# A two-layer hybrid decoder: first layer's split, results kept in SBUF, full-array norms, and a moved dense step

## The chip, the cores and the metric

The kernel runs on one core of a Trainium2 chip. The metric is the time of one execution in microseconds on the device, the median of several runs. The names of the engines are those of the profile: PE is TensorE's matmul, PEld its weight load, DVE is VectorE, ACT is ScalarE, POOL is GpSimd, SP is SyncE, whose queue issues most transfers.

## The reference

A trunk of two layers works on x (512 tokens of 1024 channels, float32) and a memory of 256 rows. Each layer adds two things to the running state h: a mixer of the normalised h, and a cross attention to the memory.

```python
un = rmsnorm(h, mix_norm_g[l])
z = un @ w_in[l]                     # 1024 x 10384: everything below is cut from z
y_rw  = rwkv7(token_shift(r, k, v, w_lo, a_lo), ...)   # 8 heads of 64, a state of 64 x 64 per head
y_gla = gla(q, k, v, f_lo)           # gated linear attention, 4 heads, chunks of 64, rms norm at its end
y_ret = retention(q, k, v, positions)# rotary embedding, 4 heads, layer norm at its end
y_lru = rglru(x)                     # conv of width 4 and a linear recurrence
y_n   = y_n * silu(gate_n)           # each branch has its own gate
merged = sum_n sigmoid(merge_n) * (y_n @ w_branch[l, n])
h = h + merged @ w_out[l]
h = h + cross_attention(rmsnorm(h), rmsnorm(mem))
```

In RWKV-7 the keys of each head are divided by their length, `kk / max(sqrt(sum(kk * kk)), 1e-12)`, the decay is `exp(-exp(log_w))` with `w0 + tanh(w_lo) @ w2` inside, and `a = sigmoid(a0 + a_lo @ a2)`; the codes `w_lo` and `a_lo` have 64 channels each. A last RMS norm closes the trunk.

## The kernel before

Everything is kept with channels on partitions and the 512 tokens in the free dimension, so h is eight tiles of 128 x 512 (tag `hm`). Precision is float32: each operand is split into a high part and the rest (`split`, L295, ScalarE casts and VectorE subtracts), and a product is three matmuls, high by high, high by rest and rest by high (`mm3`, L283, the matmuls of L287, L288 and L289). Weights come in pieces of 512 KB by SP's queue (`wload`, L266: tile `st`, three buffers), and are split the same way (L275 on ScalarE, L276 on VectorE). "Dense" below means these matmuls, 24 for one block of 128 output channels from 1024 (a gate or a projection), 12 from 512 (a branch's output).

The order of the instructions on every engine is made by a planner at build time: it plays the program with estimated times, takes what is ready by priority (order of the text, moved by `high_priority`), and fixes each engine's queue. `issue_after(ins)` adds an edge of order alone: what is in its block stands behind `ins` on that engine. Tiles of a tag share its buffers. PSUM has four large buffers (tag `b`, `pb`) for dense sums and four small ones (tag `s`, `pss`) for everything else.

The places that the change touches:

- Head of layer 1 (L192 to L200, L369 to L374, L349 to L359, L435 to L464). x is loaded in four pieces of 256 channels, transposed (L257), copied to `hm` (L372), squared and summed for the norm (L301 on ScalarE, L304 on POOL), multiplied by the gain (L357) and split (`gain_split`). The norm's factor r goes by a matmul with ones (L311) and a reciprocal. `proj_tok` computes values with tokens on partitions, in two halves of 264 (or 256) columns, from the split without r, and multiplies by r at the end; both halves sum in the large PSUM buffers, four token blocks each. `bcast_cols` (L335) spreads r over the partitions and `norm_split` (L338) makes the normalised split `uh`, `ul`.
- Linear attention (`gla`, L516) ends with four results, which `put_y` (L507) splits into tiles of tag `m` (eight buffers) and writes to DRAM (`y_sc`) by POOL's queue; `branch(n)` (L812) loads them back into tag `yb` (eight buffers) by the same queue. Retention and the recurrence do the same; RWKV's results are split in place.
- Retention (`ret`, L638) loads the rope tables into two tiles of tag `m` (L643, L644), projects q and k, swaps their halves by transfers within SBUF (L652, four for q, four for k), applies the rotation on VectorE (L654 to L656), and projects four gates before the keys are transposed.
- The rope tables themselves are made once (`rope_tables`, L396) in tiles of tag `yb`.
- RWKV's preparation (`rwkv_prep`, L871). The squares of the keys are summed per head by a matmul in plain float32 with a 32-column selector (L902), each of four blocks j of 128 channels into its own 32 PSUM partitions. The codes' weights and the codes are split over the two halves of the partitions; per block j two matmuls take the full 128 rows (L923), two take 64 rows for the rest (L926), and two of 32 rows (L940) spread the inverse lengths over the head's channels.
- In the same loop over j the dense work of the branches is handed out by `step(n)`: five steps ahead of the scores, one at the end (`NST = (5, 1)`). A step is a gate (24 matmuls, two gates at a branch's start) or an output (12 matmuls). The scores (L969, 32 matmuls of 64 rows) wait behind the five steps by `issue_after`; then ScalarE scales the keys' tile b2 chunk by chunk (L988, eight operations), TensorE transposes it (L257, 16 of 64 columns), ScalarE copies the result out (L996), and after that stands the one step.

```python
                for c in range(8):
                    S.mul(b2[:, c], b2[:, c], PL[:, j, c:c + 1])
                ...
                        transpose(tps[q][:, c], b2[qs, c].rearrange("p x s -> p (x s)"), ident[qs, qs])
                ...
                step(NST[1])
```

Behind it come the bonus (two matmuls, L1005) and nine transposes of the values, all into small PSUM buffers, and then the next block's codes.

## Time and profile before

| | us |
|---|---|
| median of 3 runs | 1773.82 (1769.37 to 1776.67) |
| the profiled execution | 1775.84 |
| its span, first to last instruction | 1774.1 |
| PE busy | 1735.2 |
| DVE busy | 1149.7 |
| ACT busy | 805.0 |
| POOL busy | 133.3 |

Mean granted TensorE clock 0.989 of full speed. The profile is of one execution; its span is a little shorter than the device's time for it. Matmuls overlap and their ends are modelled, so TensorE counts as busy for a little time after its last start; the distance from one start to the next tells more than one matmul's duration. The chain of work that ended last is 89% PE, 5% DVE, 3% transfers and 2% ACT.

### The profile page before, as it was taken

How to read it: one execution, taken by the hardware profiler on the slowest of the kernel's cores; microseconds unless marked ns; L12 is line 12 of the kernel's file. 1: busy time of each engine (PE TensorE's matmuls, PEld its weight loads, DVE VectorE, ACT ScalarE, POOL GpSimd, SP SyncE). 2: the span in 40 equal slices, each digit the busy share in tenths (PEclk: the TensorE clock that was granted, in tenths of full speed). 3: DMA queues.
4: the chain of work that ended last, by engine and by line, in shares of the span. 5: the costliest groups of instructions: out<-in, count | busy, mean ns of one | idle time of the engine just before them, and what ended most of it. 6: DMA issues, size and time to landing. Idle time of an engine off the chain costs nothing.

```text
span 1774.1 us, 27983 instructions
## 1 busy us (share of the span) xinstructions
PE 1735.2 (98%) x10690; PEld 1435.5 (81%) x10690; DVE 1149.7 (65%) x2376; ACT 805.0 (45%) x1507; POOL 133.3 (8%) x294
## 2 busy tenths in 40 slices
PE   6999999999999999999999999999999999999998
PEld 6987877877787788989898877787777778889898
DVE  8688576576775745756576736647766658457554
ACT  5494425444322334545447743544442224335454
POOL 2010200000002000000100101100101030000002
PEclk9999999999999999999999999999999999999999
DMA  7343735345563353424333427433537335334232
GB/s 217 108 131 96 183 100 146 95 110 158 152 160 91 99 162 98 134 88 127 112 92 89 140 64 213 125 96 99 156 97 198 102 94 171 96 96 142 72 107 84
DMA packets 333126, 217.34 MB, mean 123 GB/s; under 512 B 60512, under 2 KB 306624, under 8 KB 332992
## 3 DMA queue, kind: packets, MB, share of 16 engines
q1 hardware_dynamic: 318704, 189.72, 37.3%
q0 software_dynamic: 14288, 25.83, 5.1%
q8 instruction: 84, 1.38, 0.3%
q14 instruction: 50, 0.41, 0.1%
HBM read 180.91 MB, written 31.98 MB: 120 GB/s over the span
## 4 chain that ended last, share of the span: by engine, by line
PE 89%; DVE 5%; DMA 3%; ACT 2%; issue 1%; SPq 0%; POOL 0%; DVEq 0%; ACTq 0%; POOLq 0%
PE pb L287 26%; PE pb L288 26%; PE pb L289 25%; PE ps L257 3%; DVE wl L276 1%; DMA R<-R 1%; PE ps L287 1%; PE ps L289 1%; PE ps L1140 1%; PE ps L1122 1%; PE ps L288 1%; DMA m<-rope_sc 1%; PE ps L1128 1%; PE ps L717 0%; ACT sc L988 0%
## 5 line engine op out<-in xcount | busy, mean ns | idle before, releaser
L275 ACT CAST wh<-st 128x512 fp32r<-128x512 f32 (+1 forms) x548 | 339.7, 620 | 632.0 <-PE pb L288 493.4
L276 DVE TENSOR_TENSOR wl<-st,wh 128x512 fp32r<-128x512 f32 (+1 forms) x548 | 377.2, 690 | 342.8 <-ACT wh L275 308.1
L287 PE MATMUL pb<-uh,wh 128*128 128x512 f32 x1488 | 590.1, 397 | 0.0
L288 PE MATMUL pb<-ul,wh 128*128 128x512 f32 x1488 | 589.1, 396 | 0.0
L289 PE MATMUL pb<-uh,wl 128*128 128x512 f32 x1488 | 586.8, 394 | 0.0
L287 PEld LDWEIGHTS pb<-uh,wh 128*128 128x128 f32 x1488 | 282.1, 190 | 61.9 <-issue 3.7
L288 PEld LDWEIGHTS pb<-ul,wh 128*128 128x128 f32 x1488 | 282.0, 190 | 61.7 <-issue 3.9
L289 PEld LDWEIGHTS pb<-uh,wl 128*128 128x128 f32 x1488 | 281.7, 189 | 58.9 <-issue 1.2
L287 PE MATMUL pb<-yb,wh 128*128 128x512 f32 x256 | 102.2, 399 | 0.0
L289 PE MATMUL pb<-yb,wl 128*128 128x512 f32 x256 | 102.2, 399 | 0.0
L288 PE MATMUL pb<-yb,wh 128*128 128x512 f32 x256 | 101.4, 396 | 0.0
L288 PE MATMUL pb<-wl,R 128*128 128x264 f32 (+1 forms) x256 | 73.4, 288 | 4.3 <-DVE wl L276 4.3
L287 PE MATMUL pb<-wh,R 128*128 128x264 f32 (+1 forms) x256 | 73.1, 288 | 1.2 <-ACT wh L275 1.0
L289 PE MATMUL pb<-wh,R 128*128 128x264 f32 (+1 forms) x256 | 72.9, 290 | 1.3 <-DVE R L297 1.3
L289 PEld LDWEIGHTS pb<-yb,wl 128*128 128x128 f32 x256 | 48.3, 189 | 11.2 <-issue 0.7
L288 PEld LDWEIGHTS pb<-yb,wh 128*128 128x128 f32 x256 | 48.5, 189 | 10.1
L287 PEld LDWEIGHTS pb<-yb,wh 128*128 128x128 f32 x256 | 48.4, 189 | 10.2
L288 PEld LDWEIGHTS pb<-wl,R 128*128 128x128 f32 x256 | 49.8, 195 | 4.8 <-DVE wl L276 4.5
L287 PEld LDWEIGHTS pb<-wh,R 128*128 128x128 f32 x256 | 49.2, 193 | 2.2 <-ACT wh L275 1.3
L289 PEld LDWEIGHTS pb<-wh,R 128*128 128x128 f32 x256 | 49.2, 194 | 1.7 <-DVE R L297 1.5
L845 DVE SCALAR_TENSOR_TENSOR bt<-bt,pb 128x512 f32<-128x512 f32 x48 | 32.8, 682 | 26.3 <-PE pb L289 26.2
L257 PE MATMUL ps<-ident,R 128*128 128x128 f32 (+1 forms) x184 | 31.2, 290 | 12.0 <-DMA R<-in_x 6.8
(354 smaller groups left out, 2600.7 us busy)
## 6 DMA issues: line engine op xcount, KB each, us to landing
st<-in_w_in SPq DMA_DIRECT2D x154, 512.0 KB, 3.6
st<-in_w_branch SPq DMA_DIRECT2D x32, 512.0 KB, 3.4
st<-in_xa_wkv SPq DMA_DIRECT2D x32, 512.0 KB, 3.6
y_sc<-m POOLq DMA_DIRECT2D x48, 256.0 KB, 3.1
yb<-y_sc POOLq DMA_DIRECT2D x48, 256.0 KB, 5.5
st<-in_w_out SPq DMA_DIRECT2D x16, 512.0 KB, 3.8
st<-in_xa_wq SPq DMA_DIRECT2D x16, 512.0 KB, 4.0
st<-in_xa_wo SPq DMA_DIRECT2D x16, 512.0 KB, 4.0
```

The lines of the kernel that those rows point to most:

```text
L257: PE.transpose(o, i, idn)
L275: S.copy(hi, st[:, i * n:(i + 1) * n])
L276: V.tensor_tensor(lo, st[:, i * n:(i + 1) * n], hi.bitcast(F32), op=ALU.subtract)
L287: PE.matmul(o, ah, bh, start=first and i == 0, stop=False)
L288: PE.matmul(o, ah, bl, start=False, stop=False)
L289: last_mm[0] = PE.matmul(o, al, bh, start=False, stop=last and i == n - 1)
L845: V.scalar_tensor_tensor(th[d], th[d], 1.0, o, op0=ALU.add, op1=ALU.mult)
L1122: PE.matmul(rp[QS[q], j], LR[j][:, q, 0, cs_], SV[j // 2][:, j % 2, q, cs_], start=True, stop=True)
L1128: PE.matmul(up[QS[q], j], TT[QS[q], j, cs_], rs[QS[q], j], start=True, stop=True)
L1140: PE.matmul(sp[QS[q], j], bk[:, 2 * j + q], uv[:, q, j], start=True, stop=True)
```

## The change

- Layer 1 gets its own head, `first_rows`. x's pieces are loaded in another order, with the first two weight pieces of the first projection among them. From each transposed block in PSUM ScalarE writes gain times block as the high part, VectorE subtracts to the rest straight from PSUM and copies the block to `hm`. The transposes, the casts and VectorE's two operations are each chained in order. The norm's sum comes from 16 squares with accumulation on ScalarE, straight from x. In every layer `proj_tok` runs k by k over its four token blocks, and its second half sums in the small PSUM buffers.
- Linear attention's four results are split into `yb` tiles and stay there until branch 1 takes them. The rope tables are made in `hm` tiles instead.
- The key norms: the squares are split as other operands, and eight matmuls with the full array (`gather`) sum them into one group, high part and rest on all 128 partitions. The inverse lengths hold their high part in one half of the partitions and the rest in the other, and one full matmul per block (`spread`) spreads them. The codes' rests lie in two full tiles (of tag `uv`) with zeros in the other half, so each of four matmuls per block takes the full array.
- In the loop over j the single step is issued before the transposes of the scaled keys, which stand behind its last matmul by `issue_after`.
- The constants for these selectors change their shape, a padding tile grows, and POOL's scratch for descriptors is halved.

```diff
-    spread = p[:, None] % 32 == p[None, :] // 64
-    return np.concatenate([same, spread], 1).astype(np.float32)
+    gather = (np.arange(134)[None, :] - 6) % 64 == p[:, None] // 64
+    spread = p[:, None] % 64 == np.arange(T)[None, :] // 64
+    return np.concatenate([same, gather, spread], 1).astype(np.float32)
...
-    cp.tile([P, 64], F32, name="pad0")
+    cp.tile([P, PAD0], F32, name="pad0")
...
-        for i in range(4):
-            nc.sync.dma_start(xs[i], a["x"][:, i * 256:(i + 1) * 256].rearrange("(b p) d -> p b d", p=P))
+        load_x(0)
...
+        first_w = []
+        for q in range(2):
+            st = wp.tile([P, 4, 264], F32, tag="st", bufs=3, name=nm("st"))
+            nc.sync.dma_start(st, a["w_in"][0][q * 512:(q + 1) * 512, COL["gla_v"]:COL["gla_v"] + 264].rearrange(
+                "(k p) c -> p k c", p=P))
+            first_w.append(st)
+            for i in ((1, 2), (3,))[q]:
+                load_x(i)
...
-    heads = cp.tile([P, 2, P], F32R, name="heads")
-    G.dma_start(heads, a["heads"].rearrange("p (i c) -> p i c", i=2))
+    heads = cp.tile([P, P + 134 + T], F32R, name="heads")
+    G.dma_start(heads, a["heads"])
+    same = heads[:, 0:P]
+    def gather(j):
+        return heads[:, P + 6 - 2 * j:2 * P + 6 - 2 * j]
+    def spread(j):
+        return heads[:, (j + 1) * P + 134:(j + 2) * P + 134]
...
-    hT = [ht() for _ in range(KD)]
-    for k in range(KD):
-        tp = pss()
-        for b in range(4):
-            transpose(tp[:, b * P:(b + 1) * P], xs[k // 2][:, b, (k % 2) * P:(k % 2 + 1) * P], ident)
-        (V.tensor_copy if k % HMOD == 0 else S.copy)(hT[k], tp)
+    def first_rows(gcol):
+        hT = [ht() for _ in range(KD)]
+        gh, gl = [Rt((P, 4, T), F32R) for _ in range(2)], Rt((P, 4, T), F32R)
+        hi, lo, acts = [], [], []
+        ss = tiny(16).rearrange("p (b i) -> p b i", i=4)
+        last = {}
+        def chain(eng, f):
+            with ExitStack() as es:
+                if eng in last:
+                    es.enter_context(tc.issue_after(last[eng].ins))
+                last[eng] = f()
+            return last[eng]
+        for k in range(KD):
+            uh, ul = gh[k // 4][:, k % 4], gl[:, k] if k < 4 else yb()
+            with tc.high_priority(offset=100000):
+                tp = pss()
+                for b in range(4):
+                    chain("PE", lambda: PE.transpose(
+                        tp[:, b * P:(b + 1) * P], xs[k // 2][:, b, (k % 2) * P:(k % 2 + 1) * P], ident))
+                acts.append(chain("S", lambda: S.activation(uh, tp, AF.Copy, scale=gcol[:, k:k + 1])))
+            with tc.high_priority(offset=WPRI - 500):
+                chain("V", lambda: V.scalar_tensor_tensor(ul, tp, gcol[:, k:k + 1], uh.bitcast(F32), op0=ALU.mult,
+                                                          op1=ALU.subtract))
+                chain("V", lambda: V.tensor_copy(hT[k], tp))
+            hi.append(uh)
+            lo.append(ul)
+        for i in range(4):
+            with tc.issue_after(acts[min(2 * i + 3, KD - 1)].ins):
+                for b in range(4):
+                    jk = mt((P, 256))
+                    S.activation(jk, xs[i][:, b], AF.Square, accum_out=ss[:, b, i:i + 1])
+        r = tiny(4)
+        V.tensor_reduce(r, ss, axis=AX.X, op=ALU.add)
+        S.activation(r, r, AF.Sqrt, scale=1.0 / D, bias=epst[:, 0:1])
+        V.reciprocal(r, r)
+        return hT, hi, lo, r
...
-        pi_ = yb(I32)
+        pi_ = ht(I32)
...
-            parts = [wload(w_in[q * 512:(q + 1) * 512, col + c0:col + c0 + wd], 4, wd) for q in range(2)]
-            os_ = [pb((P, wd)) for _ in range(4)]
-            for q in range(2):
+            parts = [wload(w_in[q * 512:(q + 1) * 512, col + c0:col + c0 + wd], 4, wd, None if half else staged[q])
+                     for q in range(2)]
+            os_ = [(pss if half else pb)((P, wd)) for _ in range(4)]
+            for k in range(KD):
                 for b in range(4):
                     bs = slice(b * P, (b + 1) * P)
-                    mm3(os_[b], [(gh[k][:, bs], gl[k][:, bs], parts[q][0][k % 4], parts[q][1][k % 4])
-                                 for k in range(4 * q, 4 * q + 4)], first=q == 0, last=q == 1)
+                    mm3(os_[b], [(gh[k][:, bs], gl[k][:, bs], parts[k // 4][0][k % 4], parts[k // 4][1][k % 4])],
+                        first=k == 0, last=k == KD - 1)
...
+        kept = []
         def put_y(n, j, y):
+            if n == 1:
+                kept.append((yb(), yb()))
+                split(*kept[-1], y)
+                return
...
-                hi, lo = yb(), yb()
-                if n == 0:
+                hi, lo = kept[k] if n == 1 else (yb(), yb())
+                if n == 1:
+                    pass
+                elif n == 0:
...
-            xlo = ht(F32R)
+            xlo = [sb.tile([P, T], F32R, tag="uv", bufs=3, name=nm("uv")) for _ in range(2)]
+            for i in range(2):
+                G.memset(xlo[i].bitcast(F32)[(1 - i) * 64:(1 - i) * 64 + 64], 0.0)
             for i in range(2):
                 qs, os_ = slice(i * 64, i * 64 + 64), slice((1 - i) * 64, (1 - i) * 64 + 64)
                 S.copy(xst[qs, i], lo[qs])
                 G.dma_start(xst[os_, i], xst[qs, i])
-                V.tensor_tensor(xlo[qs], lo[qs], xst[qs, i].bitcast(F32), op=ALU.subtract)
+                V.tensor_tensor(xlo[i][qs], lo[qs], xst[qs, i].bitcast(F32), op=ALU.subtract)
             LR = [Rt((P, 2, 2, T)) for _ in range(4)]
             ks = [LR[j][:, 0, 1] for j in range(4)]
             nsum = pss()
-            sqs = []
             for j in range(4):
                 kt = ks[j]
                 shift(proj(COL["rw_k"] + j * P), kt, 4 + j)
                 sq = mt()
+                sqh, sql = mt((P, T), F32R), mt((P, T), F32R)
                 S.activation(sq, kt, AF.Square, scale=pc("rw_k_k", j))
-                sqs.append(sq)
-            for j in range(4):
-                PE.matmul(nsum[32 * j:32 * j + 32], C("sel"), sqs[j], start=True, stop=True)
+                split(sqh, sql, sq)
+                for x in (sqh, sql):
+                    PE.matmul(nsum, gather(j), x, start=j == 0 and x is sqh, stop=j == 3 and x is sql)
...
-            rnh, rnl = mt((P, T), F32R), mt((P, T), F32R)
-            split(rnh, rnl, rn)
+            rnp = mt((P, T), F32R)
+            S.copy(rnp, rn)
+            V.tensor_tensor(rnp[64:128], rn[64:128], rnp[64:128].bitcast(F32), op=ALU.subtract)
...
-                for i, o in enumerate((wps, aps)):
-                    qs = slice(i * 64, i * 64 + 64)
-                    PE.matmul(o, wst[qs, i, js], xlo[qs], start=False, stop=True)
+                    PE.matmul(o, wst[:, i, js], xlo[i], start=False, stop=True)
...
-                for x in (rnh, rnl):
-                    PE.matmul(nb_, heads[32 * j:32 * j + 32, 1], x[32 * j:32 * j + 32], start=x is rnh, stop=x is rnl)
+                PE.matmul(nb_, spread(j), rnp, start=True, stop=True)
...
+                mm = step(NST[1])
                 tps = [pss((P, 8, 64)) for _ in range(2)]
-                for c in range(8):
-                    for q in range(2):
-                        qs = slice(q * 64, q * 64 + 64)
-                        transpose(tps[q][:, c], b2[qs, c].rearrange("p x s -> p (x s)"), ident[qs, qs])
+                with tc.issue_after(mm):
+                    for c in range(8):
+                        for q in range(2):
+                            qs = slice(q * 64, q * 64 + 64)
+                            transpose(tps[q][:, c], b2[qs, c].rearrange("p x s -> p (x s)"), ident[qs, qs])
                 for q in range(2):
                     bk = mt((P, 8, 64))
                     S.copy(bk, tps[q])
                     nc.sync.dma_start(bk_sc[:, :, 2 * j + q], bk)
-                step(NST[1])
...
-    h = hT
+    h = None
     for l in range(depth):
+        g_ = gcol(l, "mix_norm_g")
+        if l == 0:
+            h, gh, gl, r = first_rows(g_)
         for k in range(KD):
             nc.sync.dma_start(h_sc[l][:, k], h[k])
-        g_ = gcol(l, "mix_norm_g")
-        gh, gl, r = gain_split(h, g_)
+        if l:
+            gh, gl, r = gain_split(h, g_)
         rp = bcast_cols(r, T)
-        v_gla, ex = proj_tok(l, COL["gla_v"], gh, gl, r, extra=16)
+        v_gla, ex = proj_tok(l, COL["gla_v"], gh, gl, r, extra=16, staged=(None, None) if l else first_w)
...
-    nc = bacc.Bacc("TRN2", target_bir_lowering=False, num_devices=1, dynamic_dma_scratch_size=8192)
+    nc = bacc.Bacc("TRN2", target_bir_lowering=False, num_devices=1, dynamic_dma_scratch_size=4096)
```

## Rows read from the trace of the kernel before

**Rows 1.** The page: TensorE's line and the other engines', busy us, share, instructions.

```profile
PE 1735.2 (98%) x10690; PEld 1435.5 (81%) x10690; DVE 1149.7 (65%) x2376; ACT 805.0 (45%) x1507; POOL 133.3 (8%) x294
```

**Rows 2.** Timeline of PE, first key block: start, us, line, operation, [idle before, releaser].

```profile
351.66 0.39 PE L287 MATMUL pb<-uh,wh 128*128 128x512 f32 x1
...
354.15 0.39 PE L289 MATMUL pb<-uh,wl 128*128 128x512 f32 x1
354.47 2.06 PE L969 MATMUL ps<-R,sc 64*128 64x128 f32 x32
357.33 0.62 PE L257 MATMUL ps<-ident,sc 64*128 64x64 f32 x7 [0.80 <-ACT sc L988]
...
359.81 0.50 PE L287 MATMUL pb<-yb,wh 128*128 128x512 f32 x1
```

**Rows 3.** Windows: stretch, its us, busy by engine (count), PEclk, DMA share, GB/s.

```profile
0.00:45.00 45.00, 30.72 (x210) 28.82 (x211) 36.62 (x74) 23.70 (x40) 12.52 (x20) 0.92 0.70 215
9.00:16.00 7.00, 3.33 (x25) 2.67 (x24) 7.00 (x9) 4.92 (x9) 4.01 (x4) 0.99 0.95 311
37.00:45.00 8.00, 8.00 (x68) 8.00 (x67) 7.82 (x14) 4.51 (x8) 0.00 (x0) 1.00 0.64 188
226.00:236.00 10.00, 6.40 (x32) 4.44 (x30) 9.89 (x18) 1.11 (x2) 0.00 (x0) 0.83 0.38 112
355.00:365.00 10.00, 9.20 (x73) 6.84 (x69) 8.36 (x18) 4.61 (x13) 0.15 (x1) 1.00 0.61 147
422.00:436.00 14.00, 12.90 (x82) 10.12 (x81) 7.75 (x16) 5.17 (x13) 0.00 (x0) 0.88 0.47 114
1095.00:1104.00 9.00, 6.59 (x40) 4.61 (x39) 7.72 (x15) 1.10 (x3) 0.00 (x0) 0.81 0.49 146
1250.00:1345.00 95.00, 91.53 (x462) 71.29 (x461) 63.53 (x117) 40.20 (x82) 7.10 (x21) 0.91 0.47 125
```

**Rows 4.** Waits of PE: line, what it waited for, us in total, times, longest.

```profile
PE ps L257 <- ACT sc L988: 5.4, 6, 1.1
PE ps L257 <- DVE R L656: 5.2, 4, 1.8
...
PE ps L257 <- DVE m L982: 3.2, 2, 1.6
...
PE ps L902 <- ACT m L899: 1.0, 1, 1.0
```

**Rows 5.** Timeline of DVE, head of layer 1.

```profile
8.65 1.88 DVE L372 COPY hm<-ps 128x512 f32<-128x512 f32 x3
...
36.88 2.06 DVE L342 SCALAR_TENSOR_TENSOR m<-hm,par,ps 128x512 f32<-128x512 f32 x3
```

**Rows 6.** Timeline of PE, its first work.

```profile
6.40 4.11 PE L257 MATMUL ps<-ident,R 128*128 128x128 f32 x24 [6.40 <-DMA R<-in_x]
```

**Rows 7.** Timeline of SP's queue in retention, layer 1.

```profile
215.63 0.39 SPq L270 DMA_DIRECT2D st<-in_w_in  x1
216.07 1.34 SPq L652 DMA_DIRECT2D R<-R  x2
```

**Rows 8.** Timeline of PE, sums of the keys' squares, both layers.

```profile
278.28 1.05 PE L902 MATMUL ps<-m,cst 128*32 128x512 f32 x4
...
281.10 1.04 PE L902 MATMUL ps<-m,cst 128*32 128x512 f32 x2
...
1149.81 1.04 PE L902 MATMUL ps<-m,cst 128*32 128x512 f32 x2
```

**Rows 9.** Timeline of PE, codes and norm spread of the second and third block.

```profile
363.92 0.62 PE L923 MATMUL ps<-iv,iv 128*128 128x512 f32 x2
...
365.56 0.50 PE L288 MATMUL pb<-ul,wh 128*128 128x512 f32 x1
...
397.91 0.39 PE L923 MATMUL ps<-iv,iv 128*128 128x512 f32 x1
...
400.18 0.53 PE L287 MATMUL pb<-uh,wh 128*128 128x512 f32 x1
```

More of the change, by code (lines that the diff above doesn't have):

```diff
@@ L32 @@
 WSLOT = 640
+PAD0 = 82
 JOIN = 1
@@ L77 @@
 CONSTS = (
-    ("amask", 128), ("gmask", 128), ("sel", 32),
+    ("amask", 128), ("gmask", 128),
     ("rqw", 256), ("rkw", 4), ("rg", 2), ("inv", 1), ("sgn", 1),
@@ L100, in shape_constants @@
     put("gmask", (p[None, :] >= p[:, None]) & (p[None, :] // 64 == p[:, None] // 64))
-    i = np.arange(32)
-    put("sel", i[None, :] == p[:, None] // 64)
     gam = 1.0 - 2.0 ** (-5.0 - np.arange(4))
@@ L193, in trunk_kernel, with load_x @@
     xs = [Rt((P, 4, 256)) for _ in range(4)]
+    def load_x(i):
+        nc.sync.dma_start(xs[i], a["x"][:, i * 256:(i + 1) * 256].rearrange("(b p) d -> p b d", p=P))
     with tc.high_priority(offset=100000):
-        for i in range(4):
-            nc.sync.dma_start(xs[i], a["x"][:, i * 256:(i + 1) * 256].rearrange("(b p) d -> p b d", p=P))
+        load_x(0)
     par = [cp.tile([P, NPAR], F32, name=f"par{l}") for l in range(depth)]
@@ L264, in wtile, with stage, wload @@
             t[:, :n * w].rearrange("p (n c) -> p n c", n=n)
-    def wload(src, kk, w):
+    def stage(src, kk, w):
+        st = wp.tile([P, kk, w], F32, tag="st", bufs=3, name=nm("st"))
+        nc.sync.dma_start(st, src.rearrange("(k p) c -> p k c", p=P))
+        return st
+    def wload(src, kk, w, st=None):
         with tc.high_priority(offset=WPRI):
-            st = wp.tile([P, kk, w], F32, tag="st", bufs=3, name=nm("st"))
-            nc.sync.dma_start(st, src.rearrange("(k p) c -> p k c", p=P))
+            if st is None:
+                st = stage(src, kk, w)
             his, los = [], []
@@ L397, in rope_tables @@
         MAGIC = 1.5 * 2.0 ** 23
-        pi_ = yb(I32)
+        pi_ = ht(I32)
         nc.sync.dma_start(pi_, a["positions"].partition_broadcast(P))
-        ang = yb(F32)
+        ang = ht()
         V.tensor_copy(ang, pi_)
         V.tensor_scalar_mul(ang, ang, C("inv"))
-        ah, al = yb(F32), yb(F32)
-        ahr = yb()
+        ah, al = ht(), ht()
+        ahr = ht(F32R)
         S.copy(ahr, ang)
@@ L407, in rope_tables @@
         V.tensor_tensor(al, ang, ah, op=ALU.subtract)
-        acc = yb(F32)
+        acc = ht()
         first = True
@@ L411, in rope_tables @@
             for c in two_pi_parts():
-                t, r = yb(F32), yb(F32)
+                t, r = ht(), ht()
                 V.tensor_scalar_mul(t, pt, c)
@@ L433, in trunk_kernel, with proj_tok @@
     y_sc = [dr.tile([P, NB, 4, 2, T], F32R, name=f"y_sc{l}") for l in range(depth)]
-    def proj_tok(l, col, gh, gl, r, extra=0):
+    def proj_tok(l, col, gh, gl, r, extra=0, staged=(None, None)):
         dst = Rt((P, 4, T))
@@ L1004, in rwkv_prep @@
                 for x in (rkh, rkl):
-                    PE.matmul(bon, heads[:, 0], x, start=x is rkh, stop=x is rkl)
+                    PE.matmul(bon, same, x, start=x is rkh, stop=x is rkl)
                 bv = mt()
```

## The prediction

> **What bounds the kernel now.** I read the page's busy shares first: TensorE is busy 98% of the span, the next engine 65% [rows 1]. Time comes off only where TensorE works less, waits, or runs at the lower clock; I looked for all three. Its steady pace is the yardstick: in the dense stretch ahead of the first key block, 12 matmuls of 512 columns start between 351.66 and 354.15, 0.227 us each [rows 2]; matmuls of 264 or 256 columns go 68 in 8.0 us, 0.118 each [rows 3]. The view of TensorE's waits gives few large entries: 5.4 and 3.2 us before transposes that wait for ScalarE's L988 and VectorE's L982, 5.2 us for L656, 1.0 us for L899 [rows 4]. The windows show where the clock leaves its upper level (2.4 GHz) for the lower (1.2 GHz): the first 45 us, 226 to 236, 422 to 436, 1095 to 1104 and 1250 to 1345 [rows 3]. A mean clock of 0.88 over 14 us means 0.12 x 14 = 1.7 us of full-speed work lost. All these places are touched by the change.
>
> **Part 1, the head of layer 1 (L369 to L374, L1387 to L1391).** In its first 45 us TensorE issues 210 matmuls [rows 3]: 168 of the first projection (19.8 us at 0.118), 32 transposes and 10 small ones (some 2.8 us together). So 45 - 22.6 = 22.4 us are lost there. The cause is VectorE, full from 9 to 16 us [rows 3]: each of the eight 128-row groups takes a copy, a multiply and a subtraction, and ACT and POOL a square and an add. After the change VectorE does a fused multiply-subtract (the three of L342, which also read PSUM, take 2.06: 0.66 apart) and the copy (the three of L372 take 1.88: 0.60 apart) [rows 5], 1.26 us per group, and four weight subtractions, 0.6 each by the same pitch: 12.5 us. The first transposes start at 6.40 [rows 6]; with some 1.1 us for four of them and the way to VectorE it starts at 7.5 and ends at 20.0; TensorE follows group by group and ends the first half some 1.4 us (12 x 0.118) later, at 21.4, with 96 x 0.118 + 32 x 0.056 = 13.1 us of work done: 8.3 us lost. x's last quarter arrives behind 3.7 MB (x, two weight tiles, a `heads` tile 0.27 MB larger, small ones); at the 311 GB/s of [rows 3] that is 12 us from about 2.5, so 14.5, ahead of the time at which VectorE needs it. The norm is now 16 squares on ScalarE and a reduction; they fit behind the second half (11.3 us), whose sums move to the small PSUM buffers and so don't wait for the first half's. I add 3 us for a lower clock at the start and for late pieces: 11 lost in place of 22.4, gain 11. Bounds: 14 (nothing late) and 4 (the second half still waits for the norm's PSUM buffer, or the last transposes stand ahead of the projection in TensorE's queue and wait for x until 14.5).
>
> **Part 2, linear attention's results stay in SBUF (L507 to L512, L816 to L821).** Per layer this takes 8 writes and 8 reads of 256 KB from POOL's queue, 4.2 MB. They fall where retention's half-swaps (L652) travel on SP's queue: two of these issue only at 216.07, behind a weight load at 215.63 [rows 7] that waits for VectorE, which itself waits for the rope tables, whose tiles (tag m) wait for the writes to drain. TensorE then stands 5.2 us for L656 in both layers together [rows 4] and falls to the lower clock: 0.17 x 10 + 0.19 x 9 = 3.4 us [rows 3]. With the traffic gone I expect the swaps about 8 us earlier, long before the gate projections that cover them end at about 226. Gain 8 of 8.6; bounds 0 (the weight load still goes first) and 10. The splits stay, only their target changes. All eight yb buffers are held until branch 1 uses them; the rope tables (moved to hm) and the codes (moved to uv) get out of their way. Branch 2's loads wait for them as now.
>
> **Part 3, RWKV key norms on the full array (L902).** The sums stand in seven pairs of matmuls over both layers, from 278.28 to 1149.81, each 1.04 to 1.05 us with its modelled end [rows 8], so 1.0 of path; a change of shape costs some 0.1 on either side of six of them (an estimate from the steps that follow, as at 359.81 in part 5). With the wait of 1.0 [rows 4] that is 7.0 + 1.2 + 1.0 = 9.2. After: 16 full matmuls, 3.6 us at 0.227. Gain 5.6; but each sum now hangs behind two more operations (a ScalarE copy and a VectorE subtraction), so a wait like L899's can recur: I take 4, bounds 0 and 6. The row with four matmuls in 1.05 us [rows 8] shows two heads' sums side by side for the price of one. The Trainium skill (TensorEngine Tiling (Array Packing), Theoretical Speedup) has that as a rule: matmuls that use a quarter of the array's columns can run up to four at once. It speaks against this edit: with all four together a layer would pay some 1.2 us, less than the 1.8 of the full array, and the part would lose 1.2 instead of gaining. The trace agrees for that one pair only; the other sums stand alone.
>
> **Part 4, RWKV codes and norm spread (L923 to L926, L940).** From 363.92 to 365.56 six matmuls take 1.64 us; for the third block 397.91 to 400.18, 2.27 us [rows 9]; each pays some 0.1 more behind. Two of four blocks are of either kind: 2 x 1.64 + 2 x 2.27 + 0.4 = 8.2 us a layer. After: five full matmuls per block, 4 x 5 x 0.227 = 4.5. Gain 3.7 a layer, 7.4 in all; bounds 5 and 8. The two half-tile memsets and subtractions are POOL and VectorE work under dense matmuls.
>
> **Part 5, a dense step ahead of the key transposes (L988 to L998).** Scores (L969) start at 354.47, transposes at 357.33, 0.80 of idle before them, and dense matmuls run undisturbed only from 359.81 [rows 2]. The transposes wait for eight scalings on ScalarE, and the planner fills in single dense matmuls, at 0.1 to 0.2 us per change of shape. Eight blocks: waits 5.4 + 3.2 = 8.6 [rows 4], and the modelled end of a matmul hides 0.2 more in each, 10.2. From 357.33 to 359.81 are 2.48 us with 16 transposes (1.0) and three dense ones (0.7): 0.8 of change-over, of which one clean entry and exit leave about 0.45: 8 x 0.35 = 2.8. Clock: 1.7 [rows 3] at 422, and 0.09 x 95 = 8.6 at 1250: 10.3. Together 23. The step is 12 matmuls (2.7 us) in four of the eight blocks (the yb row at 359.81 [rows 2] is one), 24 in the others, longer than the wait (at most 1.8), so the wait is covered entirely. What it covered before, the copies of the transposed keys (ScalarE L996) and the values' transposes, which need the PSUM buffers that these free, is now bare; the planner can take dense matmuls of the next block, but I charge 0.4 per block, 3 us, and leave 2 of the clock: gain 18. Bounds 23 and, with 1.8 us (the longest wait of [rows 4]) bare in every block and the clock as it is, 13 - 14 = -1.
>
> **Smaller edits.** PAD0 and the smaller scratch for POOL's descriptors move addresses: taken at 0, bounds -3 and 0 (POOL waits longest off the path). The whole plan of all queues is made anew; I take 3 us for waits that nobody sees in advance, bounds 0 and 10.
>
> **Sum.** 11 + 8 + 4 + 7.4 + 18 - 3 = 45. The profiled execution took 1775.8 (span 1774.1 and 1.7 around it), 2.0 above the median of 1773.8. 1775.8 - 45 = 1731; on the scale of the medians 1729.
>
> **Rivals.** *The clock's falls stay.* The page's rows show them behind waits of 1 to 1.8 us, but the one at 357 leaves the clock at 1.00 from 355 to 365 [rows 3], so it is at the margin. If the key blocks and retention keep them, 10.3 + 3.4 less the 2 already charged come back: 1741. The Trainium skill (TensorE: Matmul & The Clock Gate, Part 4: PE-mode transpose) says that transposes don't bring the clock up as other matmuls do; by that rule, with 16 transposes now in one run, the falls would stay. The trace speaks against it: from 6.40 on only transposes ran [rows 6], and from 9 to 16 us the clock was 0.99 [rows 3]. Chance 0.15.
> *Queue order.* Each engine's order is fixed by a plan made with estimated times. If x's last transposes stand ahead of the projection (gain 4 instead of 11) and the weight load still stands ahead of the swaps (0 instead of 8), the sum is 30: 1744. For it: now 24 of the 32 transposes go first [rows 6], and 215.63 shows the load ahead of the swaps [rows 7]. Against: VectorE frees the PSUM buffers late, so the transposes can't all go first. Chance 0.14.
> *No change.* The new plan gives back what the parts take, over 36 us; nothing in the profile has that size in one place. About 1770; chance 0.06.
> *Slower.* Place: the eight key blocks, where transposes, bonus, values' transposes and codes now stand in a row without a dense step. If each waits 1.8 us for L996's copies and then runs two falls of the clock (the three from 1250 to 1345 lost 8.6, 2.9 each), a block costs 1.8 + 5.8 = 7.6, 61 us in all, against 13 of waits and changes of shape gone, 10 of clock that is lost already and 30 - 3 of the other parts: 61 - 50 = 11 slower, 1785. It decides from 50 / 8 = 6.3 us a block. Against it: no block costs half of this now. Chance 0.04.
>
> **How the numbers follow.** The forecast, 1714 to 1739, has 0.57, better than that 0.04 (all upper bounds together: 61, so 1713 on the medians). The range of 8 in 10 takes in the first two rivals: 1711 to 1756. A change under 0.5% (8.9 us) can't be told from none. Faster is forecast, better, and the first two rivals: 0.90; same 0.06; slower 0.04.
>
> **What would show it.** Head: the projection's first half ending near 21 to 24 us, some 11 us fewer lost by 45. Retention: no wait for L656, clock 1.00 there. Norms and codes: 128-row matmuls 0.227 apart with no gap. Key blocks: a dense run between L969 and the transposes, no wait for L988; the clock's low windows gone from 422 and 1250 on. I am wrong if TensorE shows new waits over 1 us behind the transposed keys, or before the second half of the first projection.

## The result and the profile after

The changed kernel takes 1732.4 us (1730.4 to 1732.6) against 1775.2 for the kernel before on the same chip, a ratio of 0.976 (95% interval 0.972 to 0.979): 43 us faster, where 45 were forecast. On a second chip, beside experiments e6 to e8, it was 47 us (ratio 0.972, 0.969 to 0.976). The profiled span is 1730.5 us. The total is right, but its terms are not: the head of layer 1 gave about a third of what it was put down for, and two other parts gave more.

The page's busy line, which answers [rows 1]:

```profile
PE 1706.5 (99%) x10674; PEld 1426.1 (82%) x10674; DVE 1146.6 (66%) x2377; ACT 808.6 (47%) x1539; POOL 111.4 (6%) x259
```

TensorE was the bound and still is. Its largest waits after, for [rows 4]: line, what it waited for, us in total, times, longest.

```profile
PE ps L414 <- DMA R<-in_x: 8.0, 2, 7.0
PE ps L361 <- DVE m L359: 3.5, 1, 3.5
PE ps L278 <- DVE m L1053: 1.4, 2, 0.7
PE ps L1077 <- DVE m L1053: 1.1, 2, 0.6
PE ps L975 <- ACT m L322: 1.1, 2, 0.9
```

The waits for the old L988 and L656 are gone. L1053 is the old L982: TensorE still waits for it, but 2.5 in all and at most 0.7 at a time, in four of the eight key blocks, and no longer ahead of the key transposes but ahead of the bonus (L1077) and the values' transposes. The second row is the one to look at: one wait of 3.5 us that the kernel before didn't have. The windows of the same stages as in [rows 3] (columns as there):

```profile
0.00:45.00 45.00, 33.26 (x218) 31.46 (x219) 30.09 (x77) 27.11 (x67) 4.33 (x15) 0.92 0.67 209
27.00:36.00 9.00, 5.51 (x20) 4.50 (x21) 6.71 (x25) 6.28 (x10) 0.00 (x0) 0.62 0.60 171
166.00:178.00 12.00, 11.54 (x67) 8.23 (x66) 5.09 (x17) 3.21 (x12) 0.91 (x3) 0.72 0.27 89
222.00:232.00 10.00, 10.00 (x59) 7.99 (x60) 6.96 (x13) 2.86 (x5) 0.00 (x0) 1.00 0.45 131
300.00:460.00 160.00, 158.61 (x849) 128.95 (x848) 113.07 (x202) 73.53 (x144) 8.16 (x24) 1.00 0.47 128
...
1200.00:1330.00 130.00, 128.61 (x684) 104.40 (x681) 101.91 (x198) 57.94 (x114) 12.40 (x32) 1.00 0.61 163
```

The clock now stays at its upper level in retention (222) and through both sets of key blocks (300 to 460, 1200 to 1330). In 45 us TensorE issues 218 matmuls instead of 210: in this execution the head has hardly gained. Two stretches at the lower clock are left, one behind the new wait (27 to 36) and one in layer 1's linear attention (166 to 178), where the kernel before had none in its profile. e2 and e12 below keep the results and have none, so keeping them is not enough to cause it.

The first key block, for [rows 2]:

```profile
348.16 2.06 PE L1040 MATMUL ps<-R,sc 64*128 64x128 f32 x32
350.14 0.50 PE L313 MATMUL pb<-yb,wh 128*128 128x512 f32 x1
...
353.09 0.71 PE L278 MATMUL ps<-ident,sc 64*128 64x64 f32 x16
353.76 0.70 PE L1077 MATMUL ps<-m,heads 128*128 128x512 f32 x2
355.14 1.24 PE L278 MATMUL ps<-ident,R 128*128 128x128 f32 x9 [0.68 <-DVE m L1053]
```

Twelve dense matmuls stand between the scores and the transposes; the 16 transposes go in one run without a wait. The codes and the norm's spread of one block, for [rows 9]:

```profile
319.67 0.39 PE L997 MATMUL ps<-iv,iv 128*128 128x512 f32 x1
...
320.83 0.39 PE L313 MATMUL pb<-uh,wh 128*128 128x512 f32 x1
```

Five matmuls from 319.67 to 320.83, 0.23 each, with no step in the pace. A sum of a key's squares (L975), for [rows 8], is one such matmul too. This one stands 0.34 ahead of the next; the sums that no small wait precedes stand 0.23 ahead:

```profile
274.62 0.50 PE L975 MATMUL ps<-m,heads 128*128 128x512 f32 x1
274.96 0.40 PE L315 MATMUL pb<-uh,wl 128*128 128x512 f32 x1
```

**Lost time by stage.** To compare traces whose stages lie at different times, I give each matmul its steady distance to the next (0.227 us for 512 columns, 0.120 and 0.118 for 264 and 256, narrower ones by their columns; a transpose of 128 columns so counts about half of the 0.11 that it takes, the same in every kernel), and count the time beyond that sum between two points of equal work. The profiled executions, in us:

| stage | before | after | e6 | e7 | e8 | e10 |
|---|---|---|---|---|---|---|
| head of layer 1 | 23.8 | 22.1 | 15.0 | 19.3 | 20.1 | 21.6 |
| linear attention, layer 1 | 6.9 | 9.7 | 9.9 | 6.9 | 9.7 | 9.7 |
| retention, layer 1 | 14.6 | 8.8 | 8.8 | 15.4 | 8.8 | 8.8 |
| key norms, layer 1 | 3.1 | 1.8 | 1.8 | 1.7 | 1.7 | 3.0 |
| key blocks, layer 1 | 18.3 | 8.1 | 8.2 | 8.2 | 20.6 | 10.3 |
| up to retention, layer 2 | 18.0 | 16.9 | 17.3 | 16.8 | 18.1 | 17.0 |
| retention and norms, layer 2 | 23.4 | 16.0 | 15.5 | 22.9 | 15.2 | 18.9 |
| key blocks, layer 2 | 32.7 | 15.7 | 15.7 | 15.6 | 25.7 | 17.9 |
| the rest | 7.9 | 7.9 | 8.0 | 8.0 | 8.0 | 8.0 |

Before to after: 1.7 in the head, 27.2 in the key blocks, 13.2 in retention with layer 2's norms, 1.3 in layer 1's norms, 1.1 between; 2.8 given back in linear attention; and 1.9 less work. Together 43.6, as the spans differ.

### The profile page after: what moved, and what is told of

Same layout as the page of the kernel before. It is cut to its first block, busy times and chain, and to the rows that moved or that the text cites. A ratio compares the mean times of both kernels' runs of the same rounds, so it can differ in the third digit from the quotient of the medians.

```text
span 1730.5 us, 27917 instructions
## 1 busy us (share of the span) xinstructions
PE 1706.5 (99%) x10674; PEld 1426.1 (82%) x10674; DVE 1146.6 (66%) x2377; ACT 808.6 (47%) x1539; POOL 111.4 (6%) x259
## 4 chain that ended last, share of the span: by engine, by line
PE 94%; DVE 3%; ACT 1%; DMA 1%; issue 0%; SPq 0%; POOL 0%; ACTq 0%; POOLq 0%; DVEq 0%
PE pb L313 26%; PE pb L314 26%; PE pb L315 26%; PE ps L278 2%; PE ps L313 2%; PE ps L315 2%; PE ps L314 2%; PE ps L1040 1%; PE ps L1194 1%; DVE wl L302 1%; PE ps L1212 1%; PE ps L1200 1%; PE ps L784 1%; DVE R L1048 0%; PE ps L673 0%
## 5 line engine op out<-in xcount | busy, mean ns | idle before, releaser
L899 ACT ACTIVATE bt<-pb 128x512 f32<-128x512 f32 x64 | 37.9, 593 | 4.0 <-DVE hm L911 3.2
L313 PE MATMUL ps<-wh,R 128*128 128x256 f32 (+1 forms) x128 | 37.9, 296 | 0.2 <-DVE m L524 0.2
L314 PE MATMUL pb<-wl,R 128*128 128x256 f32 (+1 forms) x128 | 36.9, 293 | 0.0
L314 PE MATMUL ps<-wl,R 128*128 128x256 f32 (+1 forms) x128 | 36.9, 289 | 0.0
L313 PE MATMUL pb<-wh,R 128*128 128x256 f32 (+1 forms) x128 | 36.7, 291 | 0.0
L314 PE MATMUL pb<-iv,wh 128*128 128x256 f32 x128 | 36.6, 286 | 0.0
L313 PE MATMUL pb<-wh,uh 128*128 128x256 f32 x128 | 36.3, 284 | 0.0
```

Of the source, the lines that this page charges most:

```text
L313: PE.matmul(o, ah, bh, start=first and i == 0, stop=False)
L314: PE.matmul(o, ah, bl, start=False, stop=False)
L899: S.activation(t, o, AF.Tanh, scale=0.5)
```

## The experiments

e1 to e4 put one part alone on the kernel before (22 runs of it beside them, 1767 to 1791); e7 to e10 take one part out of the changed kernel, e5. "Loses" always means the lost time of the table.

**e1, Part 1 alone**

```diff
-    hT = [ht() for _ in range(KD)]          # all of x is transposed first, then the norm, then gain_split
+    def first_rows(gcol): ...               # rounding and rest straight from PSUM, squares from x
-            os_ = [pb((P, wd)) for _ in range(4)]
+            os_ = [(pss if half else pb)((P, wd)) for _ in range(4)]
```

> The kernel before with Part 1 alone (first_rows, the staged first weights, the sums of the second half in the small PSUM buffers). TensorE's order over its first 300 instructions is that of the changed kernel. Theory, from the trace of the changed kernel: the matmul that spreads the row factors (ones against the diagonal of r) stands ahead of the projection's second half, waits about 3.5 us for r, and the clock falls to its lower level behind it; the lost time of the first 45 us goes only from 22.5 to some 20.5, so about 2 us faster than before (0 to 4). Rival, the prediction's term: 11 us faster, the loss seen in the changed kernel being the other parts' doing.

Measured: 1775.1, ratio 0.9961 (0.9928 to 0.9993), 1 to 13 us faster. Too wide to tell 2 from 11, since the kernel before spreads over 24 us; in the profile the head loses 21.5 against 23.8, which is the theory's 2. e9 tells more.

**e2, Part 2 alone**

```diff
+            if n == 1:
+                kept.append((yb(), yb()))
+                split(*kept[-1], y)
+                return
-        pi_ = yb(I32)
+        pi_ = ht(I32)
```

> The kernel before with Part 2 alone (linear attention's results kept in SBUF, the rope tables in the other tiles). Theory (the prediction's term): no wait of TensorE for the half-swaps, the clock at its upper level from 226 to 236 and from 1095 to 1104, 8 us faster (5 to 9). Rival: keeping the results disturbs linear attention itself, where the changed kernel shows a new half-speed stretch from 169 to 176 us; then that stretch is here too and 3 us of the 8 are given back, 5 us faster. Second rival: the weight load still stands ahead of the swaps, wait and time as before, 0 us.

Measured: 1762.8, ratio 0.9889 (0.9843 to 0.9936), 11 to 28 us faster: more than any of the three. Linear attention loses 6.8 in it, as before, so keeping the results doesn't disturb that stage; the rival falls.

**e3, Parts 3 and 4 alone**

```diff
-                PE.matmul(nsum[32 * j:32 * j + 32], C("sel"), sqs[j], start=True, stop=True)
+                for x in (sqh, sql):
+                    PE.matmul(nsum, gather(j), x, start=j == 0 and x is sqh, stop=j == 3 and x is sql)
-                    PE.matmul(o, wst[qs, i, js], xlo[qs], start=False, stop=True)
+                    PE.matmul(o, wst[:, i, js], xlo[i], start=False, stop=True)
```

> The kernel before with Parts 3 and 4 (key norms, codes and norm spread on the full array). Theory (the prediction's terms): 4 for the norms and 7.4 for the codes, 11 us faster (6 to 14). Rival: the longer way to each sum of squares (a copy and a subtraction more) brings waits of TensorE that take the norms' share back, 7 us faster.

Measured: 1768.7, ratio 0.9942 (0.9915 to 0.9969), 10 us with 5 to 15. As predicted; the rival's 7 is inside the interval.

**e4, Part 5 alone**

```diff
+                mm = step(NST[1])
                 tps = [pss((P, 8, 64)) for _ in range(2)]
+                with tc.issue_after(mm):
...
-                step(NST[1])
```

> The kernel before with Part 5 alone (a dense step ahead of the key transposes). Theory (the prediction's term): no wait for the scalings of L988 or L982, no half-speed stretches from 422 and from 1250 on, 18 us faster (15 to 23). Rival: the falls of the clock belong to the narrow matmuls of norms and codes as well and stay in part while these are as before; then the 10 us of clock come back only by half, 13 us. Second rival: what stood behind the step is bare, waits for the transposed keys' copies, 0 us or slower.

Measured: 1755.4, ratio 0.9855 (0.9813 to 0.9898), 18 to 33 us faster. The key blocks lose 10.3 and 17.8 instead of 18.3 and 32.7; in its profile the falls of the clock there are gone with this part alone, so both rivals fall.

**e5, the changed kernel beside e6 to e8**

> The changed kernel itself, beside the next three on one chip, so that each can be set against it. Every theory: 1730 to 1733.

Measured: 1730.4 (1728.1 to 1731.3), the kernel before 1777.7.

**e6, the spreading matmul behind the second half**

```diff
-        rp = bcast_cols(r, T)
         v_gla, ex = proj_tok(...)
+        rp = bcast_cols(r, T, behind=last_mm[0])     # issue_after the last matmul of the projection
```

> The changed kernel with one matmul of layer 1 moved: the spreading of the row factors (ones against the diagonal of r) is issued behind the first projection's second half. Theory: the wait of 3.5 us and the half-speed stretch from 29 to 36 us both go, since TensorE has 11 us of matmuls that need no r; 7 us faster than the changed kernel (1724), and the lost time of the first 45 us falls from 20.7 to some 13.5, near the 11 that the prediction had. Rival: r's way (squares, sum, table load, root) is hidden, but the fall of the clock comes from the first 27 us and stays; 3.7 us faster. Second rival: the wait moves to the end of the second half, where the sums' buffers wait for r; no change.

Measured: 1726.2 (1723.9 to 1726.8), 4.2 below e5, in runs that don't overlap. Its windows, and the place where the spreading now stands:

```profile
0.00:45.00 45.00, 37.16 (x278) 36.13 (x279) 31.96 (x99) 27.10 (x67) 4.37 (x15) 1.00 0.74 232
27.00:36.00 9.00, 9.00 (x77) 9.00 (x76) 6.68 (x31) 6.12 (x10) 0.00 (x0) 1.00 0.46 128
```

```profile
38.20 1.12 PE L364 MATMUL ps<-m,ones 128*128 128x512 f32 x2
```

Wait and fall are both gone: 278 matmuls in the first 45 us instead of 218, and the head loses 15.0. The theory's mechanism holds, but its 7 was too much: 4.2 is nearer to the rival's 3.7, though not for the rival's reason, since the fall is gone. The 7 came from one profile of the changed kernel, and the fall behind the wait isn't always that long. The changed kernel, e5 and e7 have the same TensorE order throughout and the same wait of 3.5 before the spreading; here are 27 to 36 us in e5 and in e7:

```profile
27.00:36.00 9.00, 6.40 (x35) 5.67 (x36) 7.27 (x18) 5.68 (x10) 0.00 (x0) 0.81 0.50 144
27.00:36.00 9.00, 5.83 (x43) 5.39 (x44) 7.66 (x23) 6.10 (x11) 0.00 (x0) 1.00 0.73 223
```

The clock is 0.62 there in the first profile, 0.81 in e5 and 1.00 in e7, and the head loses 22.1, 20.2 and 19.3. So e6 saves the wait of 3.5 always and the fall sometimes.

**e7, Part 2 undone**

```diff
-                hi, lo = kept[k] if n == 1 else (yb(), yb())
+                hi, lo = yb(), yb()                  # and put_y writes n == 1 to DRAM again
```

> The changed kernel with Part 2 undone (linear attention's results go through DRAM again, the rope tables in the old tiles); TensorE's order is the same instruction by instruction. Theory: the waits for the half-swaps and the falls of the clock behind them come back in both layers, 12 us slower than the changed kernel (from the stage's lost time, 14.5 and 16 against 8.7 and 9.4). Rival, the prediction's term: 8 us slower. Second rival: what the single edit gave on the kernel before was mostly other stages' falls of the clock; in the changed kernel these are gone, and it costs 5 us or less.

Measured: 1744.2 (1740.1 to 1747.1), 13.8 slower than e5. The wait and the windows of retention, as [rows 4] and [rows 3] had them before:

```profile
PE ps L278 <- DVE R L717: 6.9, 4, 2.8
```

```profile
222.00:236.00 14.00, 10.26 (x55) 7.13 (x55) 10.86 (x23) 1.49 (x3) 0.00 (x0) 0.76 0.32 95
1076.00:1090.00 14.00, 9.59 (x54) 6.83 (x52) 10.71 (x21) 2.11 (x4) 0.00 (x0) 0.76 0.37 108
```

The transfers issued from 195 to 215 us (KB each, median us to landing) say why, first e7, then the changed kernel:

```profile
yb<-y_sc POOLq DMA_DIRECT2D x8, 256.0 KB, 7.9
y_sc<-m POOLq DMA_DIRECT2D x7, 256.0 KB, 4.3
...
R<-R SPq DMA_DIRECT2D x4, 128.0 KB, 11.1
```

```profile
R<-R SPq DMA_DIRECT2D x8, 128.0 KB, 3.8
```

A half-swap of 128 KB needs 11.1 us (median) beside POOL's writes and reads and 3.8 without them. The swaps are also issued later. SP's queue at the last of them, first e7, then the changed kernel, and below them the wait of e7's rope tables (L704) on this queue:

```profile
211.04 0.39 SPq L289 DMA_DIRECT2D st<-in_w_in  x1
211.48 1.51 SPq L713 DMA_DIRECT2D R<-R  x2
```

```profile
213.23 0.59 SPq L719 DMA_DIRECT2D R<-R  x1
```

```profile
SPq L704 <- DMA y_sc<-m: 4.4, 1, 4.4
```

The whole stage is earlier in e7, because that execution lost less before it: its first swap is issued at 188.8, that of the changed kernel at 194.4. From the first swap on, e7 reaches its last swaps after 22.7 us and the changed kernel its last after 18.8. In e7 the rope tables' load waits 4.4 us for linear attention's writes, VectorE 4.9 us for the tables, and the weight load at 211.04 for VectorE; in the changed kernel neither VectorE nor the tables' load waits for a transfer there. TensorE's order is the same in both kernels, so the transfers make the difference: 4 us of later issue and 7 us of slower landing. VectorE then waits until 220.6 for a swap. By these numbers either of the two alone would have brought it at least some 4 us forward, more than the 2.8 that TensorE waited in this layer (an estimate); the runs don't separate them.

**e8, Part 5 undone**

```diff
-                mm = step(NST[1])
-                with tc.issue_after(mm):             # around the 16 transposes
...
+                step(NST[1])                         # behind the copies of the transposed keys
```

> The changed kernel with Part 5 undone (the dense step behind the key transposes again). Theory: waits for L988 and L982 as in the kernel before and the falls of the clock from the first key block on, 18 us slower than the changed kernel (15 to 23). Rival: with norms and codes on the full array the clock stays up, and only waits and changes of shape come back, 11 us slower.

Measured: 1752.9 (1747.5 to 1754.8), 22.5 slower than e5. Its waits and its key blocks:

```profile
PE ps L278 <- DVE m L1053: 5.3, 4, 1.6
...
PE ps L278 <- ACT sc L1059: 3.2, 4, 0.8
```

```profile
300.00:460.00 160.00, 155.72 (x792) 125.76 (x791) 108.55 (x193) 71.11 (x137) 6.47 (x17) 0.96 0.43 118
1200.00:1350.00 150.00, 145.72 (x763) 117.66 (x762) 109.58 (x213) 63.02 (x126) 12.35 (x32) 0.98 0.56 152
```

Waits and lower clock are back, with norms and codes on the full array: the rival falls. The key blocks lose 46.3 against 23.8 after.

**e9, Part 1 undone**

```diff
+    hT = [ht() for _ in range(KD)]          # the old head again; everything else as in the changed kernel
-            h, gh, gl, r = first_rows(g_)
```

> The changed kernel with Part 1 undone (all of x first, transposes and the split of layer 1 as before). Theory: Part 1 as it stands gives 2 to 4 us (lost time at the projection's end 22 to 24 against 18.8 and 20.7 in two profiles of the changed kernel), so 3 us slower than the changed kernel. Rival, from the single edit on the kernel before (0.9961, interval down to 0.9928) and the prediction's term: 7 to 11 us slower.

Measured: 1733.1 (1732.1 to 1735.1), 2.7 slower than e5 (e9 to e12 ran on another chip; the kernel before has 1778.1 there, 1777.7 beside e5). Two chips make 2.7 uncertain by a few us (against the kernel before on each chip the ratios are 0.9751 here and 0.9722 for e5, 5 us apart, with intervals that overlap). The profiles say 4: the five with the old head (before, e2, e3, e4, e9) lose 23.3 to 25.3 in it, 24.3 in the mean, the seven with the new head and the spreading ahead (after, e1, e5, e7, e8, e10, e11) 18.4 to 22.1, 20.5 in the mean. So the theory's 2 to 4, not the 7 to 11. The old head waits 3.3 us for VectorE's subtraction of a weight's high part, which Part 1 did relieve.

**e10, Parts 3 and 4 undone**

```diff
-                    PE.matmul(nsum, gather(j), x, ...)
+                PE.matmul(nsum[32 * j:32 * j + 32], C("sel"), sqs[j], start=True, stop=True)   # and codes in halves
```

> The changed kernel with Parts 3 and 4 undone (key norms, codes and norm spread in quarter and half arrays). Theory, the prediction's terms: 4 + 7.4 = 11 us slower than the changed kernel. Rival: most of what the single edit gave were falls of the clock that the dense step now prevents by itself; then only the changes of shape count, 5 us slower or less. Second rival: without them the falls come back in the key blocks beside the step, 14 us or more.

Measured: 1740.2 (1737.5 to 1742.2), 9.8 slower than e5. The clock is at its upper level in the key blocks all the same, so this is the price of the shapes and of the wait shown with e11, near the prediction; both rivals fall. (e5 ran on another chip, but the stages of the two profiles give the same.) By stage: 3.9 for the norms (3.0 against 1.8; 18.9 against 16.2, the mean of 16.0 in the profile after and 16.4 in e5), and 4.4 of lost time in the key blocks with 1.9 of work, 6.3, for codes and spread.

**e11, the four sums side by side in the kernel of e10**

```diff
-            for j in range(4):
-                PE.matmul(nsum[32 * j:32 * j + 32], C("sel"), sqs[j], start=True, stop=True)
+                if j == 0:                           # behind the first projection of r
+                    mm = last_mm[0]
+                    for i in range(4):
+                        with tc.issue_after(mm.ins), tc.high_priority(offset=100000):
+                            mm = PE.matmul(nsum[32 * i:32 * i + 32], C("sel"), sqs[i], start=True, stop=True)
```

> The kernel of e10 with the four sums of squares of a layer (128x32 matmuls into the four column groups) issued one behind the other in place of scattered among the projections (all four in layer 2, three and one in layer 1). Theory: column groups run side by side, as the one pair in the kernel before did, so a layer's four cost about one matmul and one change of shape, some 1.2 us against the 4 x (0.23 + 0.2 to 0.6) of the scattered ones: 2 to 4 us faster than e10, and in the layer 2 stage as good as the full array. Rival: they run one after the other, 4 x 0.23 + 0.3, and only changes of shape are saved, 1 us or less.

Measured: 1735.1 (1730.9 to 1735.6), 5.1 faster than e10. Layer 2's sums on PE, first e10, then e11 (each sum is two records):

```profile
1123.47 1.04 PE L962 MATMUL ps<-m,cst 128*32 128x512 f32 x2
1125.39 1.05 PE L962 MATMUL ps<-m,cst 128*32 128x512 f32 x2 [0.88 <-ACT m L959]
1126.37 0.50 PE L304 MATMUL pb<-uh,wh 128*128 128x512 f32 x1
```

```profile
1121.62 1.33 PE L968 MATMUL ps<-m,cst 128*32 128x512 f32 x8
1122.88 0.50 PE L304 MATMUL pb<-uh,wh 128*128 128x512 f32 x1
```

A lone sum holds TensorE for 0.98 us (1125.39 to 1126.37), four together for 1.26 (1121.62 to 1122.88), less than the 8 x 0.227 = 1.8 of the full-array form. This is the 1.2 that the prediction worked out beside the Trainium skill's rule (TensorEngine Tiling (Array Packing), Theoretical Speedup: four quarter-array matmuls at once); the trace now agrees with it for four. In layer 2 the scattered sums took 1.9 with the wait, and three times 0.98, 4.9 in all, so 3.6 are saved; in layer 1 one run of 0.98 less; and three to four changes of shape fewer. That is 4.6 of the measured 5.1; the changes of shape may be the rest. A kernel with packed sums beside the full-array codes was not tried.

**e12, the spreading behind in both layers**

```diff
-            rp = bcast_cols(r, T, last_mm[0])        # layer 1 alone
+        rp = bcast_cols(r, T, last_mm[0])            # both layers
```

> The kernel of e6 with the spreading matmul behind the second half in layer 2 too, where the trace of the changed kernel shows one wait of 1.0 us ahead of the row factors. Theory: 1 us faster than e6 (1725). Rival: the sums of the norm themselves wait there and not their spreading, so no change from e6 (1726).

Measured: 1725.2 (1722.0 to 1727.0), ratio to the kernel before 0.9701 (0.9672 to 0.9731); e6 had 0.9699 (0.9665 to 0.9733). The 1 us can't be told apart. Against e9, on the same chip, e12 is 8.0 faster: that is Part 1 with its spreading out of the way. Either beats both kernels of the case.

## Why the prediction was right, and where it was not

| part | predicted | taken out of the changed kernel | alone on the kernel before |
|---|---|---|---|
| 1, head | 11 | 2.7 | 7 (1 to 13) |
| 2, results kept | 8 | 13.8 | 20 (11 to 28) |
| 3 and 4, norms, codes | 11.4 | 9.8 | 10 (5 to 15) |
| 5, dense step | 18 | 22.5 | 26 (18 to 33) |
| replanning | -3 | | |
| sum | 45 | 48.8 | 63 |

Taken out one by one, the parts give 48.8; all together they gave 47.3 beside e6 to e8 (1777.7 to 1730.4), so they add up within a few us. The right total came from errors of opposite sign, Part 1 too large and Parts 2 and 5 too small, and that is luck as far as the size goes.

**Part 1, the term that was mis-sized: 11 expected, 3 to 4 measured (2.7 by the medians, 3.8 by the profiles), at or below the lower bound of 4.** The step that failed is "they fit behind the second half" of the norm. The squares and the sum were done by 26.7, about when the first half ended. But the root's table load and the reciprocal came after a weight cast on ScalarE, and the matmul that spreads the factors (L361) stood in TensorE's queue ahead of the second half, which needs none of it. PE, then ACT, then DVE in the changed kernel:

```profile
26.25 0.69 PE L315 MATMUL pb<-wh,yb 128*128 128x264 f32 x4
30.49 2.04 PE L361 MATMUL ps<-m,ones 128*128 128x512 f32 x2 [3.55 <-DVE m L359]
```

```profile
26.98 0.63 ACT L301 CAST wh<-st 128x528 fp32r<-128x528 f32 x1 [0.59 <-PE pb L315]
27.63 1.28 ACT L430 ACT_TABLE_LOAD   x1
```

```profile
26.65 0.17 DVE L429 TENSOR_REDUCE ti<-ti 128x4 f32<-128x16 f32 x1
...
29.26 0.18 DVE L431 RECIPROCAL ti<-ti 128x4 f32<-128x4 f32 x1 [0.90 <-ACT ti L430]
```

The prediction named this sign ("before the second half of the first projection"), and its lower bound had a wait for the norm, but through a PSUM buffer and without the fall of the clock behind it. e6 shows what the wait costs: 4.2. With it out of the way Part 1 gives 8.0 (e12 against e9); the other 3 are missing mainly in the first half: it ended at 26.7, not 21.4. TensorE's first rows:

```profile
7.01 1.94 PE L414 MATMUL ps<-ident,R 128*128 128x128 f32 x8 [7.01 <-DMA R<-in_x]
9.93 1.97 PE L414 MATMUL ps<-ident,R 128*128 128x128 f32 x8 [0.97 <-DMA R<-in_x]
11.55 0.57 PE L313 MATMUL pb<-wh,R 128*128 128x264 f32 x1
...
12.36 0.42 PE L314 MATMUL pb<-wl,R 128*128 128x264 f32 x1
12.57 0.42 PE L313 MATMUL pb<-wh,R 128*128 128x264 f32 x1
...
15.50 0.28 PE L313 MATMUL pb<-wh,R 128*128 128x264 f32 x1
```

x's second quarter came at 9.9, and the projection began at 11.55; I had let it follow VectorE from 7.5 on. Until about 15.3 its matmuls start 0.21 to 0.23 apart, the lower clock's pace, and 0.12 after that. That VectorE alone would set the end was wrong: from 11.55 to 26.7 TensorE has no wait over 0.25, and VectorE's last subtraction ends beside it, at 26.1. Up to there 26.8 - 13.3 = 13.5 us are lost, where the sum had 8.3 and an allowance of 3. The sum also took 0.056 for a transpose; they start 0.21 apart up to 11.5 and 0.11 apart at the upper clock, so 32 of them cost at least 1.7 more than it had.

**Part 2: mechanism right, size too small (8, measured 13.8).** In the changed kernel there is no wait for the swaps, the clock is 1.00 in layer 1's retention, and there is no fall in layer 2's, as said. I had the price from one execution, where the clock was low for 3.4 us in each layer; in e7's it was low for 6.8, from 226.4 to 233.2 and from 1079.7 to 1086.6, and the stage loses 6.6 and about 6.9 more than after. TensorE's waits were longer too, 6.9 in e7 against 5.2 before. The reason that I gave holds: in e7 the tables' load waits for the writes, VectorE for the tables, the weight load for VectorE, and the last swaps stand behind it. I had left out that the swaps themselves land slower beside that traffic, 11.1 us in place of 3.8.

**Parts 3 and 4: 9.8 for 11.4**, which the stages split into about 3.9 for the norms (4) and 6.3 for codes and spread (7.4). The predicted recurrence of a wait is the L975 row above, 1.1 against 1.0 of L899. The price of four packed sums against the full array was right as well, 1.26 against 1.8.

**Part 5: 22.5 for 18.** The new waits are the L278 and L1077 rows, 2.5 in all where I charged 3 (for VectorE's L1053, and not for the copies of the transposed keys that I named), and the 2 us of clock that I left were not lost; so waits, change-over and clock together were worth 22.5 + 2.5 = 25 where I had 23. The rival by which runs of transposes keep the clock low is refuted here: each block has 16 in one run, and the clock from 300 to 460 is 1.00.

**The rivals.** The falls of the clock went in the key blocks and retention. Queue order came true for the head, but in another place: not x's transposes, but the spreading matmul. The weight load still stands ahead of the last swap (212.8 before 213.2), but TensorE no longer waits for it. The slower case needed waits of 1.8 us in every block; the longest is 0.7. Of the 3 us for replanning the runs show nothing but linear attention's 2.8, a fall of the clock that some executions have and others not (below).

## What to carry to other kernels

Look at what else stands in the bound engine's queue ahead of work that is ready: a matmul that waits for a small chain (sum, table load, root, reciprocal) costs its wait and, in five of seven profiled executions here, a fall of the clock behind it; one edge of order gave 4.2 us. Price a wait of TensorE together with the fall of the clock that follows it, and that fall from several executions, since one profile shows only one of its lengths. Traffic on another queue is worth removing not for its own time but for the buffers that it holds and the small transfers beside it that something waits for.

## What the runs showed of the hardware

The clock fell or didn't fall behind the same instructions. The head's wait of 3.5 us was followed by 6.8 us at the lower clock in the changed kernel's first profile, e1 and e10, by 3.4 in e5 and e8, and by none in e7 and e11. In linear attention the wait is short. e6 and e12 have the same TensorE order throughout layer 1, and the same short waits in linear attention (0.47 and 0.46 before L639); here are the same 12 us, first e6, then e12:

```profile
158.00:170.00 12.00, 11.52 (x70) 8.17 (x70) 6.09 (x19) 3.63 (x9) 0.31 (x1) 0.72 0.35 113
```

```profile
158.00:170.00 12.00, 11.54 (x98) 8.21 (x94) 5.58 (x19) 4.80 (x16) 0.91 (x3) 1.00 0.30 98
```

In the profiled executions that stage loses 9.7 to 9.9 in the changed kernel, e5, e6, e8, e9 and e10, and 6.8 or 6.9 in e7, e11 and e12. What decides it was not found. It fits with the spread of the runs: the kernel before, with falls in seven places of its profile, went from 1767 to 1791 us in the runs beside e1 to e4, the changed kernel from 1728 to 1733 in all of its own. That is also why the parts alone on the kernel before have wide intervals. Their sum of 63 against 47 lies within these (35 to 89); why it is higher is not shown.
